# Sigmoids of a gated recurrent unit as tanh, and stacked attention operands interleaved by four partitions, in a two-layer hybrid block

## The chip, the cores and the metric

The kernel runs on one core of a Trainium2 chip. The core has a matrix engine (TensorE, PE in the rows, with its weight loads as PEld), a vector engine (VectorE, DVE), an engine for activation functions (ScalarE, ACT), a general engine (GpSimd, POOL) and an engine that here only issues transfers (SyncE, SP). Each engine works through its own list of instructions in order and waits at an instruction until what it needs is there. Sixteen DMA engines move data between the memory on the device (DRAM) and the on-chip buffer of 128 partitions. TensorE writes into accumulators (PSUM). The metric is the device time of one execution in microseconds (us).

## The reference

Two layers work on 512 latent tokens and 256 context tokens of width 1024. In each layer the normed and modulated input is projected once and handed to four mixers of 256 channels each: a neighbourhood attention, a recurrent unit in both directions, a retention, and a differential attention. Their outputs are joined, projected, and followed by a gated feed-forward part. The two pieces that the change touches are these:

```python
def rglru_coeffs(xb, w_g, b_g, lam):
    ...
    gates = jax.nn.sigmoid(jnp.einsum('bnkc,gkcd->gbnkd', xk, w_g) + b_g[:, None, None])
    r = gates[0]...; i = gates[1]...
    log_a = -LRU_C * r * jax.nn.softplus(-lam.astype(jnp.float32))
    a = jnp.exp(log_a)
    u = jnp.sqrt(-jnp.expm1(2.0 * log_a)) * (i * xb.astype(jnp.float32))
    return a, u

def diff_core(q, k, v, lam):
    s = jnp.einsum('bqhmd,bkhmd->bhmqk', q, k).astype(jnp.float32) * (DIFF_DIM ** -0.5)
    p = jax.nn.softmax(s, axis=-1)
    a = (p[:, :, 0] - lam * p[:, :, 1]).astype(v.dtype)
    return jnp.einsum('bhqk,bkhd->bqhd', a, v)
```

The scan h = a h + u over the tokens (forward and backward) is the recurrent unit's output. LRU_C is 8. A map of the differential attention has 32 channels, and there are 8 maps.

## The kernel before

**A planner orders everything.** The kernel's Python records some 13,700 operations (`Issue.add`) with what each reads and writes, and then a list scheduler (`Issue.run`) sets the order of each engine's list and the buffer of each tile: it goes forward in a time of its own, at each step starts the operation that can start first, weighs a change of ScalarE's table, and for operations that may go to either of two engines takes the one that ends them first. So all instructions carry the line of the planner's last loop (L534), and they are told apart by their tiles: T_0 to T_25 are buffers of 1024 columns, D_0 to D_6 of 3072, t_ of 512, `s` (two, of 1024 columns) and `a` (four, of 512) are PSUM, st_ are small columns. The numbers say which buffer the planner took, so they mean nothing across two programs. A change of one operation's kind can move others.

**Precision.** Matrix products of fp32 data are made of three products in a faster format: high by high, high by low, low by high (`mm3`).

**The recurrent unit** (`lru`, step letter `l` in `ORDER`) runs in each layer over two blocks of 128 channels (`b`) and in each over two directions (`e`). For a direction, two gates are multiplied into an `s` accumulator each (six matmuls over 768 tokens) and taken out by ScalarE with a sigmoid, into `rg` and `ig`. Then come, each on 128x768: a = exp(-c r) and th = tanh(c r) on ScalarE, u = a a, th = (u + 1) th on VectorE, th = sqrt(th) on ScalarE, ig = ig x, u = th ig and the scan on VectorE. The scales c sit in the columns `cpos` and `cneg` (lines 695 and 696), the gate biases in columns 52 to 67 of `cols`. ScalarE needs a table for each kind of function. Planner and compiler count exp and tanh as one kind, and sigmoid, sqrt, silu and gelu as others; between kinds stands an ACT_TABLE_LOAD.

**The stacks of the differential attention** (`diff_stack`, letter `d`). Projected queries and keys of 128 channels (four maps of 32) are split into a high and a low part, both written to a scratch tensor `dstk` in DRAM, and read back by four transfers into one D buffer of 4 x n columns, in which the column block u is a map and the partitions hold high, high, low, low (keys) or high, low, high, low (queries) of its 32 channels: so one matmul of 128 rows adds up all four products. The issue list of SP has for each stack two writes `dstk<-T` and four reads `D<-dstk` (384 KB each with 768 columns, 256 KB with 512). There are eight stacks: keys and queries for two blocks in each of two layers. `diff_unit` then makes the scores, `s<-D_4u,D_5u` for instance, from a query stack and a key stack.

**Retention** (`ret_unit`) runs at the same time: scores `s<-T,T`, their product with a decay table on VectorE (`T_16u<-s,T_25u`), and a product with the values on TensorE.

## Time and profile before

| what | us |
|---|---|
| three runs: median (lowest to highest) | 1717.85 (1713.83 to 1718.22) |
| the profiled execution, its time | 1720.38 |
| the same, its span from first to last instruction | 1718.6 |
| TensorE (matmul) busy in it | 1642.4 |
| VectorE busy | 1248.4 |
| ScalarE busy | 831.8 |

Times in the profile are counted from the start of the span. The mean granted clock of TensorE was 0.983 of full speed. By stage: input norms and first modulation to about 43 us, mixers of layer 0 to about 500, output projection and feed-forward of layer 0 to about 1010, mixers of layer 1 to about 1310, the rest of layer 1 to the end.

### The profile page before, as it was taken

How to read it: one execution, taken by the hardware profiler on the slowest of the kernel's cores; microseconds unless marked ns; L12 is line 12 of the kernel's file. 1: busy time of each engine (PE TensorE's matmuls, PEld its weight loads, DVE VectorE, ACT ScalarE, POOL GpSimd, SP SyncE). 2: the span in 40 equal slices, each digit the busy share in tenths (PEclk: the TensorE clock that was granted, in tenths of full speed). 3: DMA queues.
4: the chain of work that ended last, by engine and by line, in shares of the span. 5: the costliest groups of instructions: out<-in, count | busy, mean ns of one | idle time of the engine just before them, and what ended most of it. 6: DMA issues, size and time to landing. Idle time of an engine off the chain costs nothing.

```text
span 1718.6 us, 26819 instructions
## 1 busy us (share of the span) xinstructions
PE 1642.4 (96%) x10511; PEld 1428.7 (83%) x10511; DVE 1248.4 (73%) x2109; ACT 831.8 (48%) x1381; POOL 173.4 (10%) x163
## 2 busy tenths in 40 slices
PE   6997999999999999999999979999999999999998
PEld 4886777576768999999987768788777899999886
DVE  4686756847679888787599998886766798777442
ACT  4377734767564434343344475854545554343221
POOL 1000101001111020200000130122111100112000
PEclk9999999999999999999999999999999999999999
DMA  9251468666464123232955553424134423332332
GB/s 378 109 148 62 142 220 245 220 225 238 157 242 175 68 80 123 77 127 94 315 179 178 199 219 104 135 87 121 37 117 147 172 99 96 102 99 87 111 124 84
DMA packets 81758, 255.14 MB, mean 148 GB/s; under 512 B 8676, under 2 KB 14148, under 8 KB 81632
## 3 DMA queue, kind: packets, MB, share of 16 engines
q1 hardware_dynamic: 81368, 253.33, 43.5%
q8 instruction: 82, 1.34, 0.3%
q14 instruction: 44, 0.36, 0.1%
q10 hardware_dynamic: 264, 0.11, 0.0%
HBM read 225.32 MB, written 28.08 MB: 147 GB/s over the span
## 4 chain that ended last, share of the span: by engine, by line
PE 76%; DVE 7%; DMA 3%; ACT 2%; issue 2%; POOL 0%; DVEq 0%; SPq 0%; POOLq 0%; ACTq 0%
PE s L534 40%; PE a L534 35%; DVE T_1u L534 1%; DVE T_15u L534 1%; DMA D_4u<-dstk 0%; DVE T_2u L534 0%; DVE T_23u L534 0%; DMA mixd<-T_24u 0%; DVE T_16u L534 0%; DMA xres<-T_24u 0%; DMA T_6u<-in_rope_dq_dram 0%; DMA rowd<-T_12u 0%; DVE T_9u L534 0%; DMA dstk<-T_4u 0%; DMA dstk<-T_15u 0%
## 5 line engine op out<-in xcount | busy, mean ns | idle before, releaser
L534 ACT ACT_TABLE_LOAD x43 | 55.2, 1283 | 24.1 <-PE s L534 8.1
L534 PE MATMUL s<-D_4u,D_5u 128*128 128x256 f32 (+1 forms) x65 | 18.1, 360 | 8.9 <-DVE T_16u L534 5.1
L534 DVE TENSOR_TENSOR st_30u<-st_30u 128x1 f32<-128x1 f32 x2 | 0.3, 161 | 31.7 <-ACT T_18u L534 23.7
L534 PEld LDWEIGHTS s<-D_4u,D_5u 128*128 128x128 f32 x65 | 10.6, 190 | 12.3 <-DVE T_16u L534 5.3
L534 POOL TENSOR_TENSOR st_5u<-st_30u,mhalf_0u 128x1 f32<-128x1 f32 (+1 forms) x4 | 4.8, 1197 | 147.0 <-DVE st_30u L534 147.0
L534 PE MATMUL a<-T_2u,D_3u 128*128 128x256 f32 x48 | 14.3, 298 | 5.3 <-ACT T_2u L534 5.3
L534 PE MATMUL a<-D_0u,T_17u 128*128 128x256 f32 (+2 forms) x64 | 18.9, 328 | 0.1
L534 PE MATMUL a<-D_0u,T_8u 128*128 128x256 f32 (+2 forms) x64 | 18.6, 325 | 0.0
L534 ACT COPY t_3u<-s 128x256 f32<-128x256 f32 (+1 forms) x14 | 5.9, 419 | 23.8 <-PE s L534 23.2
L534 PE MATMUL a<-D_2u,T_19u 128*128 128x512 f32 (+1 forms) x44 | 15.6, 355 | 0.0
L534 ACT ACTIVATE t_4u<-t_4u 128x384 f32<-128x384 f32 (+1 forms) x14 | 6.7, 478 | 17.6 <-DVE t_4u L534 17.6
L534 ACT COPY t_0u<-s 128x384 f32<-128x384 f32 (+1 forms) x11 | 4.8, 441 | 21.0 <-PE s L534 21.0
L534 ACT COPY t_5u<-s 128x384 f32<-128x384 f32 (+1 forms) x11 | 5.0, 451 | 20.7 <-PE s L534 19.9
L534 PE MATMUL a<-D_0u,T_19u 128*128 128x512 f32 (+2 forms) x44 | 14.9, 353 | 0.0
L534 PE MATMUL s<-D_3u,T_15u 128*128 128x256 f32 x64 | 14.6, 279 | 0.0
L534 PEld LDWEIGHTS a<-T_2u,D_3u 128*128 128x128 f32 x48 | 9.6, 199 | 5.6 <-ACT T_2u L534 5.5
L534 ACT COPY t_2u<-s 128x384 f32<-128x384 f32 (+1 forms) x12 | 5.3, 444 | 17.8 <-PE s L534 16.3
L534 PE MATMUL a<-T_3u,D_2u 128*128 128x256 f32 x48 | 13.9, 290 | 0.0
L534 PE MATMUL a<-D_3u,T_6u 128*128 128x512 f32 (+2 forms) x40 | 13.7, 342 | 0.0
L534 PE MATMUL a<-D_0u,T_23u 128*128 128x256 f32 (+2 forms) x48 | 13.7, 328 | 0.0
L534 PE MATMUL a<-D_0u,T_6u 128*128 128x384 f32 (+2 forms) x44 | 13.6, 338 | 0.0
L534 ACT ACTIVATE T_20u<-s 128x512 f32<-128x512 f32 x8 | 4.7, 594 | 17.8 <-PE s L534 17.3
(4178 smaller groups left out, 6743.8 us busy)
## 6 DMA issues: line engine op xcount, KB each, us to landing
D_4u<-dstk SPq DMA_DIRECT2D x16, 384.0 KB, 7.0
T_8u<-in_w_mod_dram SPq DMA_DIRECT2D x9, 512.0 KB, 9.0
T_23u<-in_w_ffn_in_dram SPq DMA_DIRECT2D x9, 512.0 KB, 4.3
T_6u<-in_w_mod_dram SPq DMA_DIRECT2D x7, 512.0 KB, 4.9
T_17u<-in_w_mod_dram SPq DMA_DIRECT2D x7, 512.0 KB, 7.1
T_14u<-in_w_ffn_out_dram SPq DMA_DIRECT2D x7, 512.0 KB, 3.9
T_20u<-in_w_mod_dram SPq DMA_DIRECT2D x6, 512.0 KB, 4.2
T_13u<-in_w_mod_dram SPq DMA_DIRECT2D x6, 512.0 KB, 6.8
```

What stands on the lines that cost most here:

```text
L534: getattr(getattr(self.real, op.eng), fn)(*map(real, a), **{x: real(v) for x, v in k.items()})
```

## The change

**Sigmoids as tanh.** sigmoid(z) = (1 + tanh(z/2)) / 2. ScalarE now makes t = tanh(0.5 z + 0.5 bias) (a new column table `hb` holds half the biases), and the rest is absorbed: exp and tanh get halved scales and, as bias, the same column again, since c r = (c/2)(1 + t). ig x becomes (t + 1) x, and u becomes (0.5 th) ig; both are a scalar-tensor-tensor operation on VectorE where a tensor-tensor operation stood, which the planner could also have given to GpSimd.

**Interleaved stacks.** The four reads of a stack now write partitions g, g+4, g+8, ... (g = 0 to 3) instead of 32 adjacent partitions each. Both stacks of a product have the same new order of rows. The planner's boxes learn a partition step, so that the four reads count as apart.

```diff
@@ class Issue, box / add
-        return p, p + dims[0][1], lo, c + sum(max(0, s * (n - 1)) for s, n in dims[1:]) + 1
+        step = max(dims[0][0] // row, 1)
+        return p, p + step * (dims[0][1] - 1) + 1, lo, c + sum(max(0, s * (n - 1)) for s, n in dims[1:]) + 1, step
...
+            hit = lambda ob: (ob[0] < box[1] and box[0] < ob[1] and ob[2] < box[3] and box[2] < ob[3] and
+                              not (ob[4] == box[4] and (ob[0] - box[0]) % box[4]))
@@ setup2
-        V.tensor_scalar(self.cpos, p[:, 16:24], 8.0, None, ALU.mult)
-        V.tensor_scalar(self.cneg, p[:, 16:24], -8.0, None, ALU.mult)
+        V.tensor_scalar(self.cpos, p[:, 16:24], 4.0, None, ALU.mult)
+        V.tensor_scalar(self.cneg, p[:, 16:24], -4.0, None, ALU.mult)
+        self.hb = c.fixed([128, 16], "hb")
+        V.tensor_scalar(self.hb, self.cols[:, 52:68], 0.5, None, ALU.mult)
@@ lru
-                    bc = self.cols[:, 52 + 8 * l + 4 * e + 2 * g + b:53 + 8 * l + 4 * e + 2 * g + b]
+                    bc = self.hb[:, 8 * l + 4 * e + 2 * g + b:1 + 8 * l + 4 * e + 2 * g + b]
...
-                    nc.scalar.activation(dst[:, 0:768], ps[:, 0:768], AF.Sigmoid, bias=bc)
+                    nc.scalar.activation(dst[:, 0:768], ps[:, 0:768], AF.Tanh, bias=bc, scale=0.5)
...
-                nc.scalar.activation(av[:, n], rg[:, n], AF.Exp, scale=cn)
-                nc.scalar.activation(th[:, n], rg[:, n], AF.Tanh, scale=cp)
+                nc.scalar.activation(av[:, n], rg[:, n], AF.Exp, scale=cn, bias=cn)
+                nc.scalar.activation(th[:, n], rg[:, n], AF.Tanh, scale=cp, bias=cp)
...
-                self.tt(ig[:, n], ig[:, n], xb[:, n], ALU.mult)
-                self.tt(u[:, n], th[:, n], ig[:, n], ALU.mult)
+                V.scalar_tensor_tensor(ig[:, n], ig[:, n], 1.0, xb[:, n], ALU.add, ALU.mult)
+                V.scalar_tensor_tensor(u[:, n], th[:, n], 0.5, ig[:, n], ALU.mult, ALU.mult)
@@ diff_stack
-                nc.sync.dma_start(big[32 * g:32 * g + 32].bitcast(F32),
+                nc.sync.dma_start(big[g::4].bitcast(F32),
```

**What the planner makes of it.** TensorE's 9633 instructions are the same ones; their order differs only in the mixers of the two layers. ScalarE's list falls from 43 table loads to 26: in the recurrent unit, from its first sigmoid up to and with the load that follows it for other work, layer 0 goes from 13 to 6 and layer 1 from 15 to 7. VectorE's 128x768 tensor-tensor operations fall from 70 to 54, and its 128x768 scalar-tensor-tensor operations rise from 42 to 58.

The first place is ScalarE's list in layer 0, at the second block of the recurrent unit. `s_80`, `s_81` are the accumulators of the gates; a tile that is its own input is the sqrt. Before:

```order
L534 ACT_TABLE_LOAD
L534 ACTIVATE T_13u_1687<-s_81,cols_0u_153 128x768
L534 ACTIVATE T_8u_1698<-s_80,cols_0u_153 128x768
L534 ACT_TABLE_LOAD
L534 ACTIVATE T_12u_1706<-T_13u_1687,cneg_0u_735 128x768
L534 ACTIVATE T_20u_1727<-T_13u_1687,cpos_0u_730 128x768
L534 ACT_TABLE_LOAD
L534 ACTIVATE T_1u_1732<-s_81,cols_0u_153 128x768
L534 ACT_TABLE_LOAD
L534 ACTIVATE T_20u_1727<-T_20u_1727 128x768
L534 ACT_TABLE_LOAD
L534 ACTIVATE T_8u_1751<-s_80,cols_0u_153 128x768
```

Now, from the same place on:

```order
L536 ACTIVATE T_14u_1690<-s_81,hb_0u_160 128x768
L536 ACTIVATE T_16u_1703<-T_14u_1690,cneg_0u_738 128x768
L536 ACTIVATE T_17u_1709<-s_80,hb_0u_160 128x768
L536 ACTIVATE T_12u_1713<-T_14u_1690,cpos_0u_733 128x768
L536 ACTIVATE T_6u_1723<-s_81,hb_0u_160 128x768
L536 ACT_TABLE_LOAD
L536 ACTIVATE T_12u_1713<-T_12u_1713 128x768
L536 ACT_TABLE_LOAD
L536 ACTIVATE T_12u_1742<-s_80,hb_0u_160 128x768
L536 ACTIVATE T_16u_1754<-T_6u_1723,cneg_0u_738 128x768
L536 ACTIVATE T_19u_1759<-T_6u_1723,cpos_0u_733 128x768
L536 ACT_TABLE_LOAD
```

Up to the fourth gate five loads stood, now two; in the whole stretch, up to the load for the softmax that follows, eight and now four.

The second place is VectorE's list at the same time. `T_8u<-T_8u,T_6u` is ig x, the 128x512 rows out of `s_81` are the retention's product with its decay table, on which TensorE waits. Before:

```order
L534 TENSOR_TENSOR T_8u_1698<-T_8u_1698,T_6u_1168 128x768
L534 TENSOR_TENSOR T_0u_1719<-T_17u_1336,T_7u_883 64x768 x2
L534 TENSOR_TENSOR T_22u_1734<-T_12u_1706 128x768
L534 SCALAR_TENSOR_TENSOR T_20u_1727<-T_22u_1734,T_20u_1727 128x768
L534 TENSOR_TENSOR T_22u_1734<-T_20u_1727,T_8u_1698 128x768
L534 SCALAR_TENSOR_TENSOR T_13u_1687<-T_12u_1706,T_22u_1734 128x256
L534 SCALAR_TENSOR_TENSOR T_13u_1687<-T_12u_1706,T_13u_1687,T_22u_1734 128x512
L534 TENSOR_TENSOR T_12u_1757<-T_17u_1336,T_7u_883 64x768 x2
L534 TENSOR_TENSOR T_8u_1751<-T_8u_1751,T_6u_1168 128x768
L534 TENSOR_TENSOR T_16u_1768<-s_81,T_25u_737 128x512
L534 TENSOR_TENSOR T_15u_1772<-T_22u_1759 128x768
L534 TENSOR_TENSOR T_16u_1768<-s_81,T_25u_737 128x512
```

Now, with one row more ahead of the second product:

```order
L536 SCALAR_TENSOR_TENSOR T_17u_1709<-T_17u_1709,T_22u_1199 128x768
L536 SCALAR_TENSOR_TENSOR T_12u_1713<-T_2u_1711,T_12u_1713 128x768
L536 TENSOR_TENSOR T_20u_1727<-T_0u_1336,T_7u_886 64x768 x2
L536 SCALAR_TENSOR_TENSOR T_2u_1711<-T_12u_1713,T_17u_1709 128x768
L536 SCALAR_TENSOR_TENSOR T_14u_1690<-T_16u_1703,T_2u_1711 128x256
L536 SCALAR_TENSOR_TENSOR T_14u_1690<-T_16u_1703,T_14u_1690,T_2u_1711 128x512
L536 TENSOR_TENSOR T_2u_1752<-T_0u_1336,T_7u_886 64x768 x2
L536 SCALAR_TENSOR_TENSOR T_12u_1742<-T_12u_1742,T_22u_1199 128x768
L536 TENSOR_TENSOR T_4u_1769<-T_16u_1754 128x768
L536 TENSOR_TENSOR T_22u_1771<-s_81,T_25u_740 128x512
L536 SCALAR_TENSOR_TENSOR T_19u_1759<-T_4u_1769,T_19u_1759 128x768
L536 TENSOR_TENSOR T_22u_1771<-s_81,T_25u_740 128x512
```

The row ahead of these is u = a a (`T_2u_1711<-T_16u_1703`). The work is the same, but the second direction's th = (u + 1) th has moved ahead of the second product.

The third place is SP's list at the last key stack (layer 1, second block). Before:

```order
L534 DMA T_18u_10545<-in_w_in_dram 128x1024
L534 DMA dstk<-T_7u_10625 128x768
L534 DMA dstk<-T_15u_10646 128x768
L534 DMA T_9u_10676<-in_w_in_dram 128x1024
L534 DMA D_4u_10686<-dstk 32x4x768 x4
L534 DMA mixd<-T_11u_10208 128x512
```

Now:

```order
L536 DMA T_24u_10558<-in_w_in_dram 128x1024
L536 DMA dstk<-T_14u_10611 128x768
L536 DMA dstk<-T_24u_10641 128x768
L536 DMA D_4u_10654<-dstk 32x4x768 x2
L536 DMA T_19u_10673<-in_w_in_dram 128x1024
L536 DMA D_4u_10654<-dstk 32x4x768 x2
L536 DMA mixd<-T_1u_10226 128x512
```

A weight load stood ahead of the four reads of the stack and stands now between the second and the third. In the program it waits for TensorE and ScalarE, whose last use frees its buffer.

## Rows read from the trace of the kernel before

**Rows 1.** The page's head and its busy times by engine.

```profile
span 1718.6 us, 26819 instructions
...
PE 1642.4 (96%) x10511; PEld 1428.7 (83%) x10511; DVE 1248.4 (73%) x2109; ACT 831.8 (48%) x1381; POOL 173.4 (10%) x163
```

**Rows 2.** Busy time by stretch; the columns stand in the first row.

```profile
core 0: us, PE busy (x) PEld busy (x) DVE busy (x) ACT busy (x) POOL busy (x), PEclk, DMA share, GB/s
43.00:150.00 107.00, 106.71 (x753) 95.95 (x752) 70.34 (x147) 59.90 (x94) 1.53 (x1) 1.00 0.32 103
150.00:172.00 22.00, 13.14 (x89) 8.49 (x88) 16.74 (x30) 18.34 (x19) 0.00 (x0) 0.87 0.37 120
172.00:193.00 21.00, 20.55 (x150) 17.13 (x151) 15.09 (x25) 14.85 (x25) 3.19 (x1) 0.89 0.34 112
193.00:279.00 86.00, 85.05 (x600) 66.12 (x599) 56.41 (x101) 38.06 (x71) 9.27 (x8) 0.96 0.68 217
279.00:301.00 22.00, 20.43 (x122) 16.68 (x121) 11.03 (x18) 12.80 (x19) 0.00 (x0) 1.00 0.77 235
301.00:516.00 215.00, 204.88 (x1319) 149.97 (x1320) 143.56 (x266) 138.81 (x275) 18.47 (x19) 0.98 0.62 216
1032.00:1160.00 128.00, 124.33 (x769) 106.67 (x768) 110.60 (x191) 83.00 (x117) 17.78 (x11) 1.00 0.35 107
1160.00:1181.00 21.00, 18.21 (x141) 15.42 (x140) 13.40 (x18) 5.89 (x11) 9.62 (x12) 0.92 0.71 208
1181.00:1310.00 129.00, 121.88 (x850) 101.47 (x850) 92.81 (x188) 73.18 (x134) 14.45 (x10) 0.96 0.26 87
```

**Rows 3.** Timeline of PE at five places: start, duration, work, [idle before].

```profile
162.25 0.94 PE L534 MATMUL s<-T_17u,T_15u 64*128 64x128 f32 x12 [2.75 <-ACT T_1u L534]
...
172.45 0.79 PE L534 MATMUL s<-D_4u,D_5u 128*128 128x512 f32 x1 [5.12 <-DVE T_16u L534]
...
287.60 0.94 PE L534 MATMUL s<-D_6u,D_4u 128*128 128x512 f32 x4 [1.57 <-DMA mixd<-T_24u]
...
1095.23 0.93 PE L534 MATMUL s<-D_4u,D_5u 128*128 128x512 f32 x4 [1.66 <-DMA T_6u<-in_rope_dq_dram]
...
1176.41 1.05 PE L534 MATMUL s<-D_4u,D_6u 128*128 128x512 f32 x3 [1.33 <-DMA D_4u<-dstk]
```

**Rows 4.** Timeline of DVE, 156 to 172.5 us.

```profile
156.93 0.96 DVE L534 TENSOR_TENSOR T_8u<-T_8u,T_6u 128x768 f32<-128x768 f32 x1
158.56 1.91 DVE L534 TENSOR_TENSOR T_0u<-T_17u,T_7u 64x768 f32<-64x768 f32 x2 [0.67 <-PE s L534]
...
161.57 0.96 DVE L534 SCALAR_TENSOR_TENSOR T_20u<-T_22u,T_20u 128x768 f32<-128x768 f32 x1
164.38 0.96 DVE L534 TENSOR_TENSOR T_22u<-T_20u,T_8u 128x768 f32<-128x768 f32 x1 [1.85 <-ACT T_20u L534]
...
171.71 0.68 DVE L534 TENSOR_TENSOR T_16u<-s,T_25u 128x512 f32<-128x512 f32 x1
```

**Rows 5.** Timeline of ACT in the same stretch.

```profile
153.91 1.28 ACT L534 ACT_TABLE_LOAD   x1 [0.51 <-PE s L534]
...
158.22 0.94 ACT L534 ACTIVATE T_12u<-T_13u,cneg_0u 128x768 f32<-128x768 f32 x1
...
163.50 0.84 ACT L534 ACTIVATE T_20u<-T_20u 128x768 f32<-128x768 f32 x1
...
174.16 1.28 ACT L534 ACT_TABLE_LOAD   x1
```

**Rows 6.** Transfers, 278 to 290 us: GB/s in 40 equal slices; issues and time to landing.

```profile
GB/s 369 164 10 0 215 82 246 348 348 246 215 246 276 215 195 174 225 246 184 225 256 205 266 307 205 215 205 277 372 413 420 437 423 437 423 437 410 369 410 410
...
D_4u<-dstk SPq DMA_DIRECT2D x4, 384.0 KB, 7.2
```

**Rows 7.** The tile D_4u, 1164 to 1178 us: its reads.

```profile
DMA to landing us min/median/max: 6.9/7.2/7.4
```

**Rows 8.** What SP's queue waited for: us in total, times, longest.

```profile
SPq L534 <- PE a L534: 440.0, 121, 28.0
```

More of the change, by code (lines that the diff above doesn't have):

```diff
@@ L203, in box @@
             lo = ap.offset + sum(min(0, s * (n - 1)) for s, n in dims)
-            return 0, 1, lo, ap.offset + sum(max(0, s * (n - 1)) for s, n in dims) + 1
+            return 0, 1, lo, ap.offset + sum(max(0, s * (n - 1)) for s, n in dims) + 1, 1
         p, c = divmod(ap.offset, row)
         lo = c + sum(min(0, s * (n - 1)) for s, n in dims[1:])
-        return p, p + dims[0][1], lo, c + sum(max(0, s * (n - 1)) for s, n in dims[1:]) + 1
+        step = max(dims[0][0] // row, 1)
+        return p, p + step * (dims[0][1] - 1) + 1, lo, c + sum(max(0, s * (n - 1)) for s, n in dims[1:]) + 1, step
     def any(self, *alts):
@@ L238, in add @@
                 box = self.box(v, None)
-            hit = lambda ob: ob[0] < box[1] and box[0] < ob[1] and ob[2] < box[3] and box[2] < ob[3]
+            hit = lambda ob: (ob[0] < box[1] and box[0] < ob[1] and ob[2] < box[3] and box[2] < ob[3] and
+                              not (ob[4] == box[4] and (ob[0] - box[0]) % box[4]))
             if w:
@@ L250, in add @@
                             op.pre.add(o)
-                            if box[0] <= ob[0] and ob[1] <= box[1] and box[2] <= ob[2] and ob[3] <= box[3]:
+                            if box[4] == 1 and box[0] <= ob[0] and ob[1] <= box[1] and box[2] <= ob[2] and ob[3] <= box[3]:
                                 continue
```

## The prediction

> **What bounds the kernel now.** I read the page's busy times first: TensorE is busy for 1642.4 of 1718.6 us, ScalarE for less than half of them [rows 1]. So 76 us of the span are not TensorE work, and a change that leaves TensorE's 9633 instructions as they are can only win some of those, or some of what a lower clock costs. ScalarE's time counts only where TensorE ends up waiting for it. The reader should therefore look at the busy times stretch by stretch, in the two mixer stages, which alone the change reorders. Beside the table loads of the first recurrent block (layer 0, about 89 to 121 us) TensorE is busy for 106.71 of 107 us; beside those of layer 1 (about 1054 to 1115 us) it lies in a stretch that is busy for 124.33 of 128 us [rows 2]. The one bad stretch beside table loads is 150 to 172 us: 13.14 of 22 us, with a mean granted clock of 0.87 there and 0.89 in the stretch behind [rows 2].
>
> The timelines of the engines in that stretch come next. TensorE waits 2.75 us at 162.25 for a sigmoid, and 5.12 us up to 172.45 for VectorE's T_16u, the retention's product, which frees an `s` accumulator [rows 3]. VectorE is not slow there, it is in order: from 156.93 on it works through the recurrent unit, waits 0.67 us for TensorE and 1.85 us for ScalarE's sqrt, and only then reaches the two products, the second of which ends at 172.39 [rows 4]. ScalarE meanwhile makes eight table loads of 1.28 us between 153.91 and 175.44 [rows 5].
>
> The last view is that of transfers. TensorE waits 1.57, 1.66 and 1.33 us at 287.60, 1095.23 and 1176.41 [rows 3]. All three are the first scores from a new stack. In two of them the trace names a transfer that TensorE doesn't read; what it reads there is D_4u, so I take the stack's reads as what came last. These reads are slow in a telling way: four of 384 KB, 1.57 MB together, land 7.2 us after issue (median), and while they run the DMA moves about 225 GB/s, whereas the weight loads behind them, which write all 128 partitions, run at 410 to 437 [rows 6]. In layer 1 it is the same, 6.9 to 7.4 us to landing [rows 7].
>
> **The change, part by part.**
>
> *Table loads.* 17 loads less are 17 x 1.28 = 21.8 us of ScalarE [rows 5]. In the first block and in layer 1 I cost them at nothing: the cover is TensorE's own matmuls of other mixers, with 0.3 us of gaps in 107, and 3.7 in 128, of which 1.66 is a stack's [rows 2, 3]. Without that cover the four or so loads that go from a block would be worth up to 5 us each time.
>
> In the second block of layer 0 they count, but not all. Without the loads ahead of the gates, ScalarE comes to the fourth gate some 3 us sooner, TensorE gets its accumulators sooner, and the wait of 2.75 us goes. What is late next is VectorE, whose list up to the second product is the limit. From 156.93 to 172.39 are 15.46 us, of which it works 15.46 - 0.67 - 1.85 = 12.94. In the new list one 128x768 operation more, 0.96 us [rows 4], stands ahead of that product. If both waits go, the product ends at 156.93 + 12.94 + 0.96 = 170.83 instead of 172.39: 1.6 us. The bounds are a loss of 1.0 (the waits stay) and a gain of 2.5 (they go and the added operation falls into a gap). I take 1.6: the sqrt that VectorE waited for has lost two of the three loads that stood between the gates and it, over 2.5 us against a wait of 1.85.
>
> *Added work.* Exp and tanh get a bias column beside the scale column. An activation of 128x768 takes 0.94 us with one column and 0.84 with none [rows 5], so 16 of them cost at most 16 x 0.1 = 1.6 us of ScalarE, hidden by its idle half; in the stretch at 150 us VectorE is later than ScalarE anyway. If that cover went, four of them would cost 0.4 us. The scalar-tensor-tensor operations that replace tensor-tensor ones take the same 0.96 us [rows 4], and all 16 stood on VectorE before. `hb` is one 128x16 operation at setup. These are 0.
>
> *Stacks.* The traffic is the same. If an interleaved read runs like the loads of all partitions, 1.57 MB take 1.57/0.42 = 3.7 us instead of 1.57/0.225 = 7.0, and the stack is there 3.3 us sooner, more than any of the three waits. They are worth 1.57 + 1.66 + 1.33 = 4.56 us at most; the other five stacks are waited for nowhere, so they give nothing. The lower bound is 0: the trace has no read with a step between partitions, and the nearest rows are the two rates. Between them I take the faster one, because such a read is spread over the buffer as the weight loads are.
> [...]
>
> So I count 4.6 us. At the third of these places the new SP list puts a weight load between the second and third reads; what that can cost is a rival below. What is late next at all three is VectorE's softmax behind the same scores, as now.
>
> *Clock.* The stretches of lower clock cost (1 - 0.87) x 22 + (1 - 0.89) x 21 = 5.2 us at 150 to 193 us, and (1 - 0.92) x 21 = 1.7 us at 1160 to 1181 [rows 2]. In the first, TensorE still idles some 7 of 22 us by the working above, so I count nothing back. In the last, its idle time would fall from 2.8 to 1.5 us, about what 279 to 301 has at full clock (1.57, 1.00) [rows 2]; but the moved weight load makes that unsure, and I leave it as the upper end.
>
> *Moved work.* Everything in the two mixer stages may have got a new neighbour. Outside the waits already named, TensorE's gaps from 172 to 516 and 1032 to 1310 us add up to 22 us [rows 2]: 0.45 + 0.95 + 10.1, and 2.0 + 1.5 + 7.1. A new order keeps their cause, three engines in step with it, and rolls their sizes anew; I take 0 for the sum and 6 us either way (estimate: some fifteen waits of 1.5 us).
>
> **Sum.** 1.6 + 4.6 = 6.2 us. The profiled execution takes 1720.4 us (1718.6 of span), so 1714.2; it lies 2.5 us above the median of the three runs, on which the same sum gives 1717.85 - 6.2 = 1711.7, or 1712 us. A change of 0.3%, about 5 us, is what a measurement of this kernel can tell from none.
>
> **The rivals.**
>
> *The stacks get no faster* (the change doesn't do what it says). [...] For it: the trace shows no strided read. Against it: the waits are short, so even a part of the 3.3 us would end them. Then 1717.85 - 1.6 = 1716.3.
>
> *The queue of SP becomes the wait: slower.* At the last key stack, reads three and four stand behind a weight load that waits for TensorE and ScalarE to give up its buffer. SP's waits for TensorE are 440.0/121 = 3.6 us in the mean and up to 28.0 [rows 8], and TensorE's next scores, then its softmax, hang on the stack. For it: the list is in order, and this stack was already waited for. Against it: the low part's write must land first, and the load can use up that time. It decides for slower where the queue is held about 11 us longer than now (6.2 gained, 5.2 to be told): at 14 us, 1717.85 - 6.2 + 14 = 1726.
>
> *The clock and the gaps come back too.* The 1.7 us of the last stack and some 6 of the gaps: 1711.7 - 7.7 = 1704. For it speaks that the planner counts on reads at the full rate and now gets them; against it, that it was free to order by its own times before as well.
>
> **How the numbers follow.** Chances: my sum 0.50, no faster stacks 0.22, the queue or another new wait of that size 0.14, clock and gaps too 0.14. Each has the 6 us of moved work around it. For my sum I count 0.54 faster, 0.38 same, 0.08 slower; for the first rival 0.25, 0.55, 0.20; for the second 0.05, 0.25, 0.70; for the third 0.9, 0.1, 0. Added up: faster 0.46, same 0.36, slower 0.18. The prediction is 1712 us; the likeliest case's own range is 1705 to 1719. With no more than 2 in 10 outside, the whole range goes from the third rival less a part of its spread, 1702, to the first plus its spread and the beginning of the second, 1723.
>
> **What would show it.** Right: reads `D<-dstk` landing in about 4 to 5 us and DMA rates near 400 GB/s while they run; no TensorE wait at the first scores of a stack; 26 table loads; the retention's second product near 171 us; gaps at layer 1's table loads as small as before. Wrong: landings of 7 us again; a wait of several us for the last key stack, with SP idle ahead of its third read; or a sum of gaps in 172 to 516 and 1032 to 1310 us that differs by more than 6 us from 22, which would mean that the moved work decides and not the parts.

## The result and the profile after

The changed kernel takes 1699.72 us (median of four runs, 1697.60 to 1702.54) against 1718.03 (1713.83 to 1719.02) for the kernel before: a ratio of 0.9899, 95% interval 0.9875 to 0.9923, 18.3 us less. The direction was as predicted. The size was not: I had counted 6.2 us, and 1699.7 lies below the low end of my range, 1702. The profiled execution took 1698.05 us.

First the page's head and busy times of the changed kernel, and of its costliest groups the one of the table loads (busy us, mean ns, idle before it):

```profile
span 1696.3 us, 26782 instructions
...
PE 1631.6 (96%) x10511; PEld 1418.7 (84%) x10511; DVE 1237.5 (73%) x2105; ACT 814.3 (48%) x1370; POOL 173.8 (10%) x162
...
L536 ACT ACT_TABLE_LOAD x26 | 33.4, 1283 | 4.9 <-issue 2.2
```

TensorE runs the same 10511 matmul records as in [rows 1] and is still busy for 10.8 us less, at a mean granted clock of 0.988 instead of 0.983. The table by stretch, cut at the same times as [rows 2], shows where:

```profile
core 0: us, PE busy (x) PEld busy (x) DVE busy (x) ACT busy (x) POOL busy (x), PEclk, DMA share, GB/s
43.00:150.00 107.00, 106.98 (x756) 96.36 (x753) 70.18 (x147) 56.03 (x91) 1.29 (x1) 1.00 0.28 102
150.00:172.00 22.00, 15.83 (x107) 10.29 (x108) 19.70 (x36) 15.32 (x17) 0.00 (x0) 0.96 0.39 120
172.00:193.00 21.00, 20.25 (x145) 15.91 (x143) 14.08 (x22) 14.68 (x29) 3.20 (x1) 0.96 0.37 126
193.00:279.00 86.00, 79.20 (x571) 60.82 (x568) 48.64 (x96) 36.06 (x66) 12.78 (x9) 0.98 0.58 204
279.00:301.00 22.00, 22.00 (x125) 18.96 (x124) 10.58 (x17) 10.13 (x17) 0.00 (x0) 1.00 0.84 299
301.00:516.00 215.00, 209.22 (x1361) 151.53 (x1360) 151.18 (x277) 142.03 (x284) 15.22 (x18) 1.00 0.65 228
1032.00:1160.00 128.00, 126.12 (x816) 108.63 (x815) 103.42 (x167) 79.09 (x118) 24.33 (x14) 1.00 0.34 113
1160.00:1181.00 21.00, 21.00 (x161) 19.27 (x160) 17.25 (x33) 10.88 (x19) 8.39 (x11) 1.00 0.45 150
1181.00:1310.00 129.00, 125.12 (x855) 102.38 (x855) 90.91 (x179) 69.95 (x128) 16.81 (x12) 1.00 0.30 103
```

From 301 us on the granted clock is full in every stretch shown, where [rows 2] have 0.98, 0.92 and 0.96. One stretch is clearly worse, 193 to 279 us, where TensorE idles 6.8 us instead of 0.95. Its timeline shows what it waits for now in layer 0 (start, duration, work, [idle before]); the last row is from layer 1:

```profile
161.52 1.03 PE L536 MATMUL a<-T_19u,sT_0u 128*2 128x512 f32 x4 [1.64 <-DMA T_19u<-in_w_mod_dram]
...
168.05 1.03 PE L536 MATMUL a<-T_21u,sT_0u 128*2 128x512 f32 x4 [1.58 <-DMA T_21u<-in_w_mod_dram]
...
245.31 1.87 PE L536 MATMUL a<-T_18u,sT_0u 128*2 128x512 f32 x4 [2.72 <-DMA T_18u<-in_w_mod_dram]
...
290.27 0.87 PE L536 MATMUL s<-D_6u,D_4u 128*128 128x512 f32 x4
...
1164.95 0.85 PE L536 MATMUL s<-D_4u,D_5u 128*128 128x512 f32 x4
```

The two waits of 2.75 and 5.12 us of [rows 3] are replaced by shorter ones, now for weights of the next modulation. The last two rows are first scores from a new stack, one in each layer, without a wait. VectorE's list at the retention's product, against [rows 4]:

```profile
161.12 0.96 DVE L536 SCALAR_TENSOR_TENSOR T_2u<-T_12u,T_17u 128x768 f32<-128x768 f32 x1
...
166.99 0.95 DVE L536 TENSOR_TENSOR T_4u<-T_16u 128x768 f32<-128x768 f32 x1
167.86 0.68 DVE L536 TENSOR_TENSOR T_22u<-s,T_25u 128x512 f32<-128x512 f32 x1
168.46 0.95 DVE L536 SCALAR_TENSOR_TENSOR T_19u<-T_4u,T_19u 128x768 f32<-128x768 f32 x1
169.32 0.68 DVE L536 TENSOR_TENSOR T_22u<-s,T_25u 128x512 f32<-128x512 f32 x1
```

None of these rows waits, and the second product ends at 170.00; I had worked out 170.83. ScalarE's timeline there, against [rows 5]:

```profile
156.29 1.02 ACT L536 ACTIVATE T_12u<-T_14u,cpos_0u 128x768 f32<-128x768 f32 x1
...
158.59 1.28 ACT L536 ACT_TABLE_LOAD   x1
159.89 0.84 ACT L536 ACTIVATE T_12u<-T_12u 128x768 f32<-128x768 f32 x1
```

An activation with two columns takes 1.02 us, against 0.94 with one. The waits of SP's queue for TensorE, against [rows 8] (us in total, times, longest):

```profile
SPq L536 <- PE a L536: 402.8, 99, 33.5
```

They are fewer; the longest is 5.5 us longer, but the first scores of the three stacks no longer wait.

TensorE runs equally many matmuls in every kernel here, so a trace can be cut at matmul numbers and compared piece by piece. Worked out from the two traces, in us (idle: gaps of TensorE inside the piece; half: how long the granted clock was at 0.50 of full speed there, the only lower level in the two traces):

```
matmuls        begins   before: length, idle, half       after: length, idle, half
400 to 3400    48       469.3   22.2   23.9              463.2   18.6    6.8     mixers, layer 0
3400 to 5600   518      408.6    2.2    3.4              406.6    2.0    0.0     feed-forward
5600 to 6200   926      133.2   14.3   13.7              136.7   15.6   17.1     border of the layers
6200 to 7850   1059     259.3   14.7   13.7              243.4    5.8    0.0     mixers, layer 1
7850 to 10500  1319     390.0    1.2    0.0              388.6    1.2    0.0     rest
```

Of the 22 us between the two executions 15.9 come from the mixers of layer 1: 8.9 us less idle time, and 13.7 us less at half clock, worth about half, 6.9 (estimate: in the kernel before a 128x256 matmul starts every 0.21 us in the stretch at half clock that ends at 245.0 us, and every 0.12 us right behind it). Together they are 15.8. My sum had 3.0 there, the waits of two stacks. These are two single executions, 22 us apart where the medians are 18.3 apart.

### The profile page after: what moved, and what is told of

Its sections match the earlier page's. It is cut to its first block, busy times and chain, and to the rows that moved or that the text cites. A ratio compares the mean times of both kernels' runs of the same rounds, so it can differ in the third digit from the quotient of the medians.

```text
span 1696.3 us, 26782 instructions
## 1 busy us (share of the span) xinstructions
PE 1631.6 (96%) x10511; PEld 1418.7 (84%) x10511; DVE 1237.5 (73%) x2105; ACT 814.3 (48%) x1370; POOL 173.8 (10%) x162
## 4 chain that ended last, share of the span: by engine, by line
PE 82%; DVE 11%; issue 2%; ACT 2%; DMA 1%; POOL 0%; DVEq 0%; POOLq 0%; SPq 0%; ACTq 0%
PE a L536 42%; PE s L536 41%; DVE T_2u L536 1%; DVE T_12u L536 1%; DVE T_5u L536 1%; DVE T_14u L536 0%; DVE T_7u L536 0%; DVE T_9u L536 0%; DMA T_12u<-in_w_ffn_in_dram 0%; DVE T_19u L536 0%; DVE T_3u L536 0%; DVE T_20u L536 0%; DVE T_17u L536 0%; DVE T_4u L536 0%; DVE T_16u L536 0%
## 5 line engine op out<-in xcount | busy, mean ns | idle before, releaser
L536 PE MATMUL s<-D_6u,D_4u 128*128 128x512 f32 x64 | 17.5, 357 | 1.3 <-ACT T_17u L536 1.0
L536 PE MATMUL a<-D_0u,T_21u 128*128 128x256 f32 (+2 forms) x56 | 18.5, 330 | 0.0
L536 PE MATMUL a<-D_3u,T_21u 128*128 128x256 f32 (+2 forms) x52 | 17.6, 339 | 0.0
L536 PE MATMUL a<-D_1u,T_21u 128*128 128x256 f32 (+1 forms) x60 | 17.5, 318 | 0.0
L536 PEld LDWEIGHTS s<-D_6u,D_4u 128*128 128x128 f32 x64 | 10.8, 188 | 7.8 <-ACT T_16u L536 1.7
L536 PE MATMUL a<-D_0u,T_24u 128*128 128x512 f32 (+2 forms) x52 | 17.2, 344 | 0.0
L536 PE MATMUL a<-D_0u,T_0u 128*128 128x256 f32 (+2 forms) x56 | 16.9, 339 | 0.2 <-ACT T_20u L536 0.2
L536 PE MATMUL a<-D_0u,T_15u 128*128 128x512 f32 (+2 forms) x52 | 16.7, 346 | 0.0
L536 PE MATMUL a<-D_3u,T_24u 128*128 128x512 f32 (+2 forms) x52 | 16.5, 343 | 0.0
L536 PE MATMUL a<-D_2u,T_21u 128*128 128x256 f32 (+1 forms) x48 | 16.4, 341 | 0.0
L536 PE MATMUL a<-D_0u,T_22u 128*128 128x256 f32 (+2 forms) x56 | 15.8, 321 | 0.0
L536 ACT COPY t_0u<-s 128x384 f32<-128x384 f32 (+1 forms) x11 | 4.7, 430 | 20.1 <-PE s L536 18.3
```

The source lines that it names most:

```text
L536: getattr(getattr(self.real, op.eng), fn)(*map(real, a), **{x: real(v) for x, v in k.items()})
```

## The experiments

**Taking the change apart.** Three things changed at once: stacks, gates, and the order of every list. The planner's costs can be set so that it plans for one kind of gate while the program uses the other, so each can be had alone. Theory A: the new order brings what I had set to 0. Theory B: the table loads are worth more than counted. Theory C: the interleave is.

Interleave alone, in the order of before (sigmoids, 43 loads):

```diff
-                nc.sync.dma_start(big[32 * g:32 * g + 32].bitcast(F32),
+                nc.sync.dma_start(big[g::4].bitcast(F32),
```

> The kernel before with interleaved stacks alone; every engine's list as before. Theories A and B: only the three waits go, 4.6 us at most, so 1713 to 1714. Theory C: 10 us or more, 1708 or less. In all of them the four reads should land in 4 to 5 us where they took 7; if they land in 7 again, the interleave makes no read faster and the time is that of before.

Measured: 1709.92 us, ratio 0.9951 (0.9939 to 0.9964), 7.3 us less than the 1717.17 beside it. Between A and C. The reads of the last key stack, tile D_4u, are those of [rows 7]:

```profile
DMA to landing us min/median/max: 5.0/5.3/5.6
```

And the DMA rate from 1158 to 1170 us, in 40 equal slices:

```profile
GB/s 369 174 0 82 229 215 113 280 416 379 321 358 365 335 260 389 338 369 328 389 328 328 277 420 225 164 92 79 379 389 297 253 253 393 294 287 379 410 154 31
```

They land 1.9 us sooner, mostly at some 260 to 420 GB/s where [rows 6] have about 225. TensorE's wait of 1.33 us shrinks to 0.2, and the stretch at half clock of 3.4 us that began there at 1176.8 is gone with it: 1.1 + 1.7 us from one stack. The two other first scores that waited, at 287.60 and 1095.23 us in [rows 3], come without a wait as well. By matmul numbers the three places give 1.1, 1.9 and 2.9 us, 5.9 together.

Not all of the rest belongs to the stacks. TensorE's list is the same in both kernels. Here is one stretch of it in the kernel before and in this one (columns as in the table by stretch):

```profile
236.00:248.00 12.00, 12.00 (x90) 9.47 (x91) 5.88 (x18) 0.98 (x2) 1.99 (x1) 0.72 0.84 273
237.00:249.00 12.00, 11.61 (x112) 8.81 (x111) 7.28 (x21) 1.89 (x3) 2.70 (x1) 1.00 0.90 298
```

No stack is waited for in either, and the first has a clock of 0.72 with TensorE busy all the time. It costs some 2.5 us there. So the clock of one execution can differ where the list and the waits do not.

The reads of the last key stack land in 5.3 us where I had worked out 3.7 from the rate of the weight loads. And the reads of the stack that TensorE waited for at 287.60 us, issued from 276.70 us on in this kernel, still land in 7.2 us (median), as in [rows 6]; what ended the wait there was not shown.

The reverse, tanh with the old reads (every list as in the changed kernel):

> The changed kernel with its four reads of a stack writing 32 adjacent partitions again, every engine's list otherwise as in the changed kernel. All three theories against 1718 us before and 1700 after. Theory A (the new order of the mixers brings what I had set to 0, some 12 us): the stacks give 4.6, so 1704 to 1705. Theory B (the 17 loads are worth more than 1.6): the same 1704 to 1705. Theory C (the interleave is worth more than the three waits, by a higher clock and by what follows the scores): 1710 or more, at least 10 us above the changed kernel.

Measured: 1706.13 us (0.9937, 0.9924 to 0.9950), so the interleave is worth 6.4 in the new order. That is between what A and B had said and what C had, nearer to A and B. The largest loss in its trace is at one place, the last stack's first scores, here in the timeline of TensorE:

```profile
1173.59 0.77 PE L536 MATMUL s<-D_4u,D_5u 128*128 128x512 f32 x1 [3.21 <-DMA D_4u<-dstk]
```

And two stretches there, with the columns of the table by stretch above (busy us of each engine, PEclk behind them):

```profile
1160.00:1170.00 10.00, 10.00 (x91) 9.26 (x85) 5.49 (x11) 4.59 (x8) 5.79 (x8) 1.00 0.95 231
1170.00:1181.00 11.00, 7.79 (x24) 6.03 (x23) 2.99 (x6) 2.96 (x5) 3.79 (x3) 0.69 0.38 114
```

A wait of 3.2 us, and behind it a clock of 0.69 over 11 us, 3.4 us more. From the 6800th to the 7000th matmul this kernel loses 6.2 us against the changed one. So this wait cost about twice its length. The wait comes from slow reads and hardly from SP's queue, as the reads of D_4u in this kernel show (first and last issue, then time to landing):

```profile
L536 SPq DMA_DIRECT2D D_4u<-dstk x4: 303/403/1638, 1160.4 to 1164.4; - x4
DMA to landing us min/median/max: 7.9/7.9/7.9
```

The four are issued within 4.0 us, in the changed kernel within 3.5 (1155.1 to 1158.6), but land 2.5 us later after issue than there (5.4).

Tanh in the order of before, with interleaved stacks (30 loads):

```diff
+            if f is AF.Tanh and op.k.get("scale") == 0.5:
+                return n * 0.833 + (52 if psum else 93) + acc + 93.0 * min(cols, 2), "g"
+            if n == 768 and f in (AF.Exp, AF.Tanh) and isinstance(op.k.get("scale"), View):
+                cols = 1
```

> The order of the kernel before on every engine, interleaved stacks, gates as tanh with 30 table loads where the kernel before has 43. Theory A: 1.6 from the loads and 4.6 from the stacks, 1711 to 1713; the rest needs the new order. Theory B: the loads alone give 10 or more beside the stacks, 1703 or less. Theory C: 1708 or less, and within 2 us of the kernel that has the interleave alone.

Measured: 1707.55 us (0.9941, 0.9928 to 0.9954), 2.4 less than the interleave alone, a difference that the two intervals don't separate. Theory A said 1711 to 1713, its loads 1.6. B, with 10 or more for the loads, falls. C, with 1708 or less and within 2 us of the interleave alone, comes nearest. By matmul numbers 2.3 us are gained between the 1000th and the 1400th, at the second recurrent block of layer 0, where I had put the 1.6.

Sigmoids in the order of the changed kernel (42 loads):

```diff
+            if f is AF.Sigmoid:
+                return n * 0.833 + (52 if psum else 93) + acc + 93.0 * min(cols, 2), "e"
...
-                    nc.scalar.activation(dst[:, 0:768], ps[:, 0:768], AF.Tanh, bias=bc, scale=0.5)
+                    nc.scalar.activation(dst[:, 0:768], ps[:, 0:768], AF.Sigmoid, bias=bc)
```

> The order of the changed kernel on every engine and interleaved stacks, but the gates are sigmoids again (sigmoid, plain products, no bias columns in exp and tanh), so ScalarE has 42 table loads where the changed kernel has 26. Theory A (the order brings it): it keeps nearly all, 1701 to 1703, since the loads themselves are hidden. Theory B (the loads bring it): it loses 10 us or more against the changed kernel, 1710 to 1715. Theory C: as A, 1701 to 1703.

Measured: 1714.98 us (0.9989, 0.9977 to 1.0000), 15 more than the changed kernel. Here B seems right and A wrong: 13 loads are worth 2.4 us in the one order, 16 are worth 15 in the other. Two of the waits that come with them, and that the changed kernel doesn't have at the same matmuls, in the timeline of TensorE:

```profile
119.66 0.39 PE L540 MATMUL a<-D_0u,T_14u 128*128 128x256 f32 x1 [2.36 <-DVE T_14u L540]
...
1113.44 0.61 PE L540 MATMUL s<-D_6u,D_4u 128*128 128x512 f32 x2 [3.14 <-ACT T_1u L540]
```

The order of before was made around 43 loads and hides them. The new one was made without them, and by these waits has too little room for them. So loads and order can't be priced apart; along the chain that was measured the interleave is 7.3, the loads 2.4 and the order 7.8, together 17.5 of the 18.3 (each median has its own kernel before beside it; the step called order also takes the loads from 30 to 26).

**Is the order luck?** The planner was given one constant altered by some per cent, which says nothing on the change but draws another order, once for tanh and once for sigmoids, stacks interleaved in both. Theory S: fewer loads make any order better, by about 10 us. Theory R: it is a draw.

```diff
-        return out.shape[0] * n * 4 / 332.0, None
+        return out.shape[0] * n * 4 / 328.0, None
```

> The changed kernel planned anew with one constant of the planner altered by about 1% (its DMA rate, 332 to 328), which says nothing on the change: 26 table loads, another order. Theory S (with fewer table loads any order of this planner is better, by some 10 us against interleaved sigmoids): 1697 to 1703, and 8 to 12 below the sigmoid kernel with the same alteration. Theory R (the new order was a lucky draw; the loads alone are worth 2.4, as with the order of before): scattered by some 6 us around 1707, and on the mean over the pairs only 2 to 4 below the sigmoid kernels.

> The kernel with sigmoids and interleaved stacks planned anew with the same altered DMA rate: 43 table loads, another order. Theory S: 1707 to 1713, near the 1709.9 of its sister with the order of before. Theory R: scattered by some 6 us around 1710, so that it can come out below its tanh partner.

```diff
-MORE = {"tensor": 54.0, "scalar": 70.0, "vector": 92.0, "gpsimd": 60.0, "sync": 50.0}
+MORE = {"tensor": 54.0, "scalar": 75.0, "vector": 92.0, "gpsimd": 60.0, "sync": 50.0}
```

> The changed kernel planned anew with another constant altered (the price of an added wait on ScalarE, 70 to 75 ns). Theory S: 1697 to 1703. Theory R: anywhere from 1701 to 1713.

> Sigmoids and interleaved stacks planned anew with the same altered price of a wait. Theory S: 1707 to 1713, 8 to 12 above its tanh partner. Theory R: anywhere from 1704 to 1716, with no fixed distance to its partner.

```diff
-            return n * 0.833 + (52 if psum else 93) + acc + 93.0 * min(cols, 2), TABLE.get(f)
+            return n * 0.833 + (52 if psum else 93) + acc + 98.0 * min(cols, 2), TABLE.get(f)
```

> The changed kernel planned anew with a third constant altered (the price of a column operand on ScalarE, 93 to 98 ns). Theory S (fewer loads make any order better): 1697 to 1703. Theory R (the order is a draw): anywhere from 1701 to 1713.

> Sigmoids and interleaved stacks planned anew with the same altered price of a column. Theory S: 1707 to 1713, 8 to 12 above its tanh partner. Theory R: anywhere from 1704 to 1716, with no fixed distance to its partner.

Measured, tanh and sigmoid: 1703.37 and 1713.23 (DMA rate), 1700.03 and 1712.23 (wait), 1710.87 and 1710.56 (column). Two pairs of three go nearly as S said, the third has no difference at all, so neither theory holds. The traces showed a third: the mixers of layer 1 take 253.0 to 253.5 us in all four sigmoid kernels, 244 in the tanh kernels that are fast, and 251.2 in the one that is not. In the slow ones TensorE's list at the end of these mixers is arranged as before (I call it arrangement X), in the others as in the changed kernel (Y).

This is X, in the kernel before, in TensorE's timeline:

```profile
1232.62 0.88 PE L534 MATMUL s<-ident_0u,T_3u 128*128 128x128 f32 x6 [0.43 <-ACT T_0u L534]
1236.35 1.51 PE L534 MATMUL s<-ident_0u,T_22u 128*128 128x128 f32 x6 [2.86 <-DVE T_22u L534]
...
1271.30 0.50 PE L534 MATMUL a<-D_3u,T_16u 128*128 128x512 f32 x1 [2.10 <-DVE T_16u L534]
```

And the stretches around the two waits:

```profile
1225.00:1245.00 20.00, 16.72 (x106) 13.26 (x105) 12.69 (x23) 11.01 (x20) 2.15 (x2) 0.83 0.09 27
1262.00:1282.00 20.00, 16.66 (x125) 12.65 (x124) 15.02 (x34) 8.49 (x15) 3.30 (x2) 0.91 0.38 131
```

The transposes of one softmax (`T_3u`) and of the next (`T_22u`) stand next to each other on TensorE, while VectorE still divides the second:

```profile
1235.19 1.02 DVE L534 SCALAR_TENSOR_TENSOR T_22u<-T_0u,st_23u,T_22u 128x768 f32<-128x768 f32 x1
```

In the changed kernel 12 matmuls of a projection stand between the two, the first of them in the second row:

```profile
1220.96 0.82 PE L536 MATMUL s<-ident_0u,T_2u 128*128 128x128 f32 x6
1221.54 0.48 PE L536 MATMUL s<-D_3u,T_21u 128*128 128x512 f32 x1
...
1224.56 0.84 PE L536 MATMUL s<-ident_0u,T_19u 128*128 128x128 f32 x6
```

And the stretches that answer to those of X:

```profile
1220.00:1240.00 20.00, 18.71 (x130) 14.84 (x128) 15.21 (x33) 11.62 (x23) 3.65 (x2) 1.00 0.08 27
1245.00:1265.00 20.00, 17.41 (x139) 14.24 (x138) 17.92 (x42) 12.23 (x22) 5.51 (x4) 1.00 0.51 172
```

No wait stands at these transposes, and the clock stays full. Two shorter waits, of 1.29 and 1.41 us, are left in this end.

**Arrangement or loads?** Theory Q: the arrangement of that end gives the 8 us, whatever the gates are. Theory L: only fewer loads give them. The price of a table load in the planner, 1280 ns, was altered to get sigmoids with an end near Y, and tanh with X:

```diff
-                t += 1280.0
+                t += 1200.0
```

> Sigmoids and interleaved stacks, 43 table loads, planned anew with the planner's price of a table load at 1200 ns instead of 1280. In this plan TensorE's list at the end of layer 1's mixers stands near that of the changed kernel. Theory Q (the arrangement of that end gives the 8 us): layer 1's mixers take 244 to 247 us as in the changed kernel, where the other four sigmoid plans take 253, and TensorE's waits of 2.9 and 2.1 us there are gone. Theory L (only fewer loads give it): 253 again. In the whole, layer 0 being a draw: 1702 to 1708 by Q, 1709 to 1714 by L.

```diff
-                t += 1280.0
+                t += 1300.0
```

> The changed kernel planned anew with that price at 1300 ns: 26 table loads, and TensorE's list at the end of layer 1's mixers near that of the kernel before. Theory Q: layer 1's mixers take 251 to 253 us, with waits of about 2.9 and 2.1 us at the end, and the whole 1706 to 1712. Theory L: 244, and the whole 1698 to 1704.

Layer 1's mixers: 247.8 us for sigmoids with Y, 251.4 for tanh with X; Q had expected 244 to 247 and 251 to 253, L 253 and 244. TensorE's timeline for tanh with X:

```profile
1230.50 1.51 PE L536 MATMUL s<-ident_0u,T_17u 128*128 128x128 f32 x6 [3.10 <-DVE T_17u L536]
...
1264.38 0.79 PE L536 MATMUL a<-D_3u,T_20u 128*128 128x512 f32 x1 [2.10 <-DVE T_20u L536]
```

A stretch of it around the first of the two waits:

```profile
1220.00:1240.00 20.00, 16.71 (x110) 13.36 (x109) 12.98 (x25) 11.71 (x23) 1.30 (x2) 0.91 0.07 27
```

And the same piece of the program for sigmoids with Y:

```profile
1240.00:1260.00 20.00, 18.73 (x132) 14.82 (x131) 14.54 (x32) 11.02 (x21) 3.53 (x2) 1.00 0.08 27
```

The two waits come with X and go with Y, whatever the gates are, as Q says. But with sigmoids Y gives some 5 us, not the 8 that Q named; the rest needs fewer loads. The whole time followed only in the second kernel: 1709.45 us (0.9941, 0.9919 to 0.9964) as Q expected, but 1721.70 (1.0017, 1.0005 to 1.0029) for sigmoids with Y, outside what either theory gave, since its layer 0 takes 474.8 us where the other sigmoid plans take 463 to 471. Layer 0 was a draw of its own.

Two more tanh plans, one with a DMA rate of 334, one with the price of a wait at 75 ns and the weight of a table change at 700:

> The changed kernel planned anew with a DMA rate of 334 instead of 332, the plan that the planner itself holds for the shortest of some thirty. If its times were right to 1%, about 1693; if the plan is a draw among the tanh plans, 1700 to 1711. TensorE's list at the end of layer 1 is neither that of before nor that of the changed kernel.

> The changed kernel planned anew with two constants altered (the price of an added wait on ScalarE 75 ns, the weight of a change of table 700 ns), the end of layer 1 near the changed kernel's. Theory Q: layer 1's mixers 243 to 246 us, and the whole 1696 to 1704.

Measured: 1706.51 us (0.9924, 0.9903 to 0.9946) and 1699.24 (0.9891, 0.9866 to 0.9917). The planner's own favourite is not the fastest; no plan beats the changed kernel by more than can be told. In the first, neither wait of X is left and the clock stays full in layer 1's mixers, yet these take 248.2 us, with TensorE idle for 9.7: losing the two waits is not all that Y brings. All kernels with interleaved stacks, in us:

```
kernel                  loads  end   whole     mixers layer 0   mixers layer 1 (idle, half clock)
sigmoid, order before   43     X     1709.9    464.0            253.3 (11.6,  6.8)
sigmoid, DMA rate       43     X     1713.2    471.4            253.3 (10.7, 10.2)
sigmoid, wait           43     X     1712.2    463.5            253.5 (10.6, 10.2)
sigmoid, column         43     X     1710.6    462.7            253.0 (11.4,  6.8)
tanh, order before      30     X     1707.6    465.4            252.4 (11.2,  6.8)
tanh, column            26     X     1710.9    466.9            251.2 (10.3,  6.8)
tanh, load 1300         26     X     1709.5    465.5            251.4 (10.8,  6.8)
sigmoid, load 1200      43     Y     1721.7    474.8            247.8 ( 8.3,  0.0)
sigmoid, order after    42     Y     1715.0    472.3            248.2 ( 8.5,  3.4)
tanh, changed kernel    26     Y     1699.7    463.2            243.4 ( 5.8,  0.0)
tanh, DMA rate          26     Y     1703.4    467.0            244.4 ( 6.8,  0.0)
tanh, wait              26     Y     1700.0    464.1            244.3 ( 6.1,  0.0)
tanh, wait and weight   26     Y     1699.2    463.6            243.8 ( 5.8,  0.0)
tanh, DMA rate 334      26     other 1706.5    467.4            248.2 ( 9.7,  0.0)
```

In layer 1 the arrangement is worth about 5 us with sigmoids and 7 to 9 with tanh, fewer loads about 1 to 2 in X and 4 in Y.

Four plans of each kind were not chosen by their end: the order of before for sigmoids, the changed kernel's for tanh, and the three altered constants for both. Their means are 1703.5 us for tanh and 1711.5 for sigmoids, 8.0 apart where the first pair is 10.2 apart; the tanh plans spread from 1699.7 to 1710.9. So part of the changed kernel's gain, about 4 us against the mean of its kind, is luck of the draw.

**Is a wait dearer than its length everywhere?** In layer 1 lower clock came with X in every kernel (6.8 us or more at half), in the kernel before at its two waits (0.83 and 0.91 over 20 us). Theory K: long waits do that anywhere. Theory G: a wait costs its length. Waits were put into the changed kernel's feed-forward, eight with two copies (five copies at every second place in the other kernel):

```diff
+                x = real(op.a[0][2]["rhs"])
+                for _ in range(2):
+                    self.real.scalar.copy(x, x)
```

> The changed kernel with eight short waits put on TensorE in the feed-forward of layer 0, where it is otherwise busy: at eight places ScalarE copies a 128x384 operand of the next matmul onto itself twice (the values stay), about 1.4 us of idle TensorE each, 11 us together. Theory G (a wait costs its own length): 1700 + 11 = 1711, and the granted clock stays full in that stretch. Theory K (waits of 2 us and more bring a stretch of half clock on top, short ones don't): also 1711, the clock stays full.

> The same at four of these places with five copies each, about 2.8 us of idle TensorE each, 11 us together. Theory G: 1711 again, as with eight short ones. Theory K: each wait has 3.4 us or 6.8 us at half clock with it, so 1.7 to 3.4 us more per wait: 1718 to 1725, with four stretches of half clock in the feed-forward of layer 0.

Measured: 1708.52 us (0.9941, 0.9922 to 0.9961) and 1708.82 (0.9950, 0.9936 to 0.9965). The waits came out shorter than I had worked out: five of 0.6 to 1.2 us in the first kernel, and in the second only two of over 2 us, 2.23 and 2.62, beside 0.32 and 0.80. The two kernels cost the same, 9 us. In the feed-forward itself the traces show 7.6 and 7.1 us more, for 4.8 and 6.0 us more of idle TensorE; the first has 3.4 us at half clock there too, worth 1.7, from 550.3 us on, ahead of its first added wait. Some 2 us more of either trace lie in layer 0's mixers, ahead of all added waits. So in both the waits cost some 1.1 us more than their length in all, nearly as G says. The longest wait of the second, in TensorE's timeline:

```profile
704.66 0.62 PE L542 MATMUL s<-D_2u,T_24u 128*128 128x384 f32 x2 [2.62 <-ACT D_2u L540]
```

And the stretch around it:

```profile
690.00:720.00 30.00, 27.38 (x156) 26.84 (x156) 22.87 (x33) 11.21 (x18) 4.43 (x3) 1.00 0.28 97
```

A wait of 2.6 us and a full clock, and the same around the wait of 2.23: K falls for this stage. A wait's length alone doesn't decide about the clock: full at 2.62 us here, 0.91 over 20 us around the 2.10 of X in the kernel before.

## Why the prediction was too small, point by point

**Moved work: the step that failed.** I wrote that a new order "keeps their cause, three engines in step with it, and rolls their sizes anew", and took 0 with 6 us either way. Measured with the gates held at tanh, the order gave 7.8 us. The spread of 6 was about right, as the tanh plans show (1699.2 to 1710.9 us); the centre of 0 was not, since four of these seven plans lie 4 us or more below the 1707.6 of tanh in the order of before. And the gain is no sum of small draws. By matmul numbers layer 1's mixers give 9.0 us and layer 0's 2.2, and the border of the layers takes 5.5 back. TensorE's list at the end of layer 1's mixers has two arrangements, and the one of before has waits of 2.86 and 2.10 us with lower clock, both inside a stretch [rows 2] that shows 7.1 us idle and a clock of 0.96. I had added those 7.1 us to a pool of gaps instead of asking what each one is and what the new list puts in its place. The sign that I had named for this, a sum of gaps more than 6 us away from 22, would not have shown it: by the table after it is 19.1, since a stretch cut at fixed times doesn't hold the same work in both kernels, and since it leaves the clock out.

**Clock: counted at 0, and it was a third to a half of the gain.** I priced the clock in two places and left 193 to 279, 301 to 516 and 1181 to 1310 us out. By [rows 2] these are worth (0.04 x 86) + (0.02 x 215) + (0.04 x 129) = 12.9 us at most, since TensorE idles in part of them. All but 1.7 of it is gone after. Of the 22 us between the two executions TensorE's busy time is 10.8, and 6.9 of that lie in layer 1's mixers, where the clock was low at the waits of X and of the last stack. The 0.04 of 193 to 279 us has no such cause: it comes from the stretch at 236 us, where the same list ran at full clock with interleave alone and at 0.72 again, from 233 to 245 us, with tanh in the order of before.

**Stacks: right in direction, too small.** At the last key stack, with equal lists, the reads became faster, but by 1.9 us (7.2 to 5.3) instead of 3.3, and that was enough for the wait there. That a spread read runs at the rate of the weight loads was my estimate; what sets its rate no run shows. Counted 4.6, measured 7.3 in the old order and 6.4 in the new one. Of the 7.3 the three places show 5.9, of which 1.7 is lower clock that went with the last wait; the rest lies where no stack is waited for, and no run shows it to be the interleave's.

**Table loads: right.** Counted 1.6 us at one place and 0 elsewhere; in the order of before they gave 2.4, nearly all at that place. The nothing elsewhere held for that order alone. The warning beside it, that without cover a block's loads cost up to 5 us, is what sigmoids in the new order showed: 15 us in all.

**Added work: right.** 0.08 us more for a second column, and VectorE free of waits in the rows where an operation was added.

**The rivals.** No faster stacks: refuted at the last key stack (5.3 us to landing instead of 7.2). SP's queue at the last stack: no wait came there in the changed kernel; with slow reads the same lists do wait 3.2 us at that place, but for reads that land late, and the weight load between them holds the queue little. Clock and gaps coming back, 1704, with 14 in 100, is nearest to what happened, and more of both came back. Its reason, that the planner now gets reads at the full rate, is not: the order of before with fast reads keeps the waits of X.

Open: whether and why 26 loads lead the planner to Y more often. Of the four plans of each kind that were not chosen by their end, three for tanh have Y and none for sigmoids, which is too few to tell. The loads of layer 1's recurrent unit are past by then, so I take it that what they leave over for the end matters, but no run shows which step decides. That the projection between the transposes is what removes the wait is read from lists and traces; moving it alone wasn't tried.

## What to carry to other kernels

Where a planner sets the order, a change of one operation's price is a change of every list behind it: take the largest waits of the old trace one by one and look in the new list at what stands in their place, before calling the rest a draw. Time several plans of each variant, too: plans for the same gates lie up to 12 us apart here. To price a part alone, hold the order fixed in both directions, with the work of before in the new order too: 13 table loads cost 2.4 us in the plan made for them, and 16 cost 15 in the other. And add the clock: time below full clock in all stretches, not in the worst one, is what a removed wait can bring on top of its length (3.4 us at half clock went with a wait of 1.33 us here), but not every such stretch belongs to a wait (0.72 from 236 to 248 us with TensorE busy throughout).

## What the runs showed of the hardware

The granted clock was at half for 6.8 us or more of layer 1's mixers in all eight kernels with arrangement X: 0.83 and 0.91 over 20 us around the waits of 2.86 and 2.10 us in the kernel before, 0.91 and 0.91 around those of 3.10 and 2.10 us with tanh, load 1300. It was full throughout these mixers in the five kernels with Y and interleaved stacks that show 0.0 in the table; the longest waits there are 1.41 us in the changed kernel and 1.51 in the sigmoid one (load 1200). In the feed-forward it stayed full at waits of 2.23 and 2.62 us. In the kernel before it was 0.72 from 236 to 248 us with TensorE busy throughout, and with interleave alone 1.00 in the same list. What else is needed for it to fall was not settled.

Reads into every fourth partition, four at a time, landed in 5.3 us instead of 7.2 at the last key stack with the same lists around them (medians). In the same kernel the reads issued from 276.70 us on landed in 7.2 us, as in the kernel before.
